# Seven block products in another order on swapping banks, and the sample rows computed apart from the prompt rows

## The chip, the core and the metric

One core of one Trainium2 chip runs the whole kernel. The metric is device time in microseconds (us) of one execution. Matrix work runs on TensorE (PE), whose weight loads are listed apart (PEld); VectorE (DVE) and ScalarE (ACT) read PSUM and do the elementwise work; nearly all DMA is issued from SyncE's queue (SP).

## What is computed

One layer of a hybrid decoder, for a prompt of 2048 tokens and for 8 sample tokens (one new token of each of 8 sequences, with a cache of 2048 positions):

```
h = rms_norm(x)                               # 1024 wide
q, k, v of three dilated attention groups, 8 heads of 64      = h @ w_in[...]
att = softmax over the groups' lse of the groups' outputs, times silu(gate)
HGRN2 branch: f, q, i of 8 heads of 128 = h @ w_in[...]; a chunked scan; RMSNorm; silu gate
merged = sigmoid(ga) * (att @ w_att_proj) + sigmoid(gb) * (ho @ w_hg_proj)
y = rms_norm(x + merged @ w_out)
```

The outputs are y of the prompt and of the samples, the last keys and values, and the scan's states. Everything is float32.

## The kernel before, in words

**Projections.** All columns of w_in are projected with a Strassen form: a block of 1024 tokens (half of the prompt) by 1024 channels, times 1024 channels by two column blocks, is split in quarters and made of seven products in place of eight. The seven sums of token quarters (A11, A12, A22 and S1 to S4) are kept in SBUF for a whole half as `Hh` and `Hl` (make_H, L192); the matching sums of weights are made for each pair of column blocks by w_combos (L216). For accuracy every operand is split in a rounded part and a remainder (split_w, L188: L189 on ACT, L190 on DVE), and each product takes three matmuls per 128 channels. `ORDER` (L46) is the order in which PE takes the products; some are added up in one PSUM bank, so that a partial sum must be copied out (keep_c, ACT, L369) before the next product is added to the same bank.

**Two kinds of block.** V and I columns come out token-major (nat_block, L259: 5 blocks per half, 336 matmuls of 256 columns, L308 to L311). All others come out channel-major in pairs of 128 columns (t_pair, L350: 34 pairs per half, lines L362 to L365). In the first half (p = 0) t_pair runs each product twice, over 256 columns and then over 260, the last four of which are sample tokens: half of the samples are carried as extra columns of each token quarter. In the second half (p = 1) there is one run of 512 columns.

```
45  SETS = (((0, 256), (256, 260)), ((0, 512),))
46  ORDER = ("A11", "A12", "S2", "S3", "S1", "A22", "S4")
```

In t_pair pa takes product 0, is copied, takes 2, is copied, takes 3, is copied, takes 5; pb takes half of product 1 in front of each of the first two copies' successors; pc takes 4 and 6. The sample columns of a result are taken out by L376 or L378. In nat_block the samples are separate float32 matmuls (L267) and stores.

**Order of the work.** In program order, for p = 0: normalise and transpose 8 tiles of 128 prompt tokens and the samples (norm_T, L241; x_tile, L1109), make_H, V block 0, then 8 more tiles which are stored to hscr for the second half, `setup`, then the V blocks 1 and 2 and two I blocks. att_stage (12 pairs of q and k, with the attention of each group beside the next pair), cb_stage (4 pairs; combine; for p = 0 also the samples' attention: samp_qk, samp_score L703, samp_softmax, samp_av L743), hg_stage (8 heads, 2 pairs each). Then merge pairs 4 and 6 of p = 0, make_H for the second half, merge pair 0 of p = 1, and the samples' scan (samp_hg, L1047, and samp_hg_end). The second half repeats from the V blocks: nat_block, att_stage, cb_stage, hg_stage. At the end a flag is reduced (L1184 to L1191), an If block stands for an exact fallback, one last merge pair (6) runs, and two output stages follow (L1266 to L1268, L1300 to L1302).

**What sets the order.** The program's text is the priority. A scheduler lays the instructions of each engine out ahead of time by priority and its own estimate of when inputs are there, and each engine then runs its list strictly in order. The weight sums of t_pair are made with high priority, so they run ahead of the pair that uses them; five raw tiles (`wr`) and 7 (p = 0) or 5 (p = 1) slots of split weights (`wh`, `wl`) hold them. Tiles wait for the earlier owner of their place. PSUM has eight banks: six for products and two for the rest (`ps_side`, px) in the V and I blocks, three and five elsewhere.

## Time and profile before

| | |
|---|---|
| three runs | 3269.86, 3271.39, 3275.21 us (median 3271.39) |
| the profiled execution | 3269.79 us, its span 3268.0 us |
| busy, share of the span | PE 90%, PEld 77%, DVE 58%, ACT 45% |
| instructions | PE 20260, DVE 4622, ACT 3276 |
| mean granted TensorE clock | 0.951 |
| DMA | 347.97 MB, 106 GB/s over the span |

Times are read from the start of the span. PE is the engine with the most work, so the question of each stage is when PE isn't busy, and what it then waits for; an idle DVE or ACT costs nothing by itself.

### The profile page before, as it was taken

What the parts mean: (1) busy time and instruction counts of PE and PEld (TensorE: products, weight loads), DVE (VectorE), ACT (ScalarE), POOL (GpSimd) and SP (SyncE); (2) the same over time, 40 slices, a digit from 0 to 9 for tenths busy, and PEclk for the clock granted to TensorE, in tenths of its full rate; (3) what the DMA queues carried; (4) which work ended last, traced back from release to release, by engine and by line L of the source; (5) the groups of instructions that cost most, each with busy time, mean ns of one, the idle gap of its engine ahead of it and who ended that gap; (6) DMA issues with size and microseconds to landing.
All of it is one profiled execution on the core that took longest, in us unless ns stands there. A gap on an engine that the chain in (4) does not pass through costs nothing. (4 is left out here: it accounts for less than half of the span.)

```text
span 3268.0 us, 54030 instructions
## 1 busy us (share of the span) xinstructions
PE 2930.1 (90%) x20260; PEld 2514.7 (77%) x20260; DVE 1882.2 (58%) x4622; ACT 1474.3 (45%) x3276; POOL 2.5 (0%) x8
## 2 busy tenths in 40 slices
PE   5799999998779898963799999999899996999999
PEld 4698887887758898962798766767677775899987
DVE  7344555456856777762444555557777775544444
ACT  5322445444436666642232455445576765211222
POOL 0000000000000000000000000000000000000000
PEclk7899999998989999985899999999999998999999
DMA  3432132215732121137342232225422222755542
GB/s 127 144 130 88 52 86 72 77 57 175 236 123 69 59 78 59 60 109 155 111 146 89 74 86 81 86 73 163 134 72 73 70 80 65 218 153 145 157 141 84
DMA packets 444798, 347.97 MB, mean 106 GB/s; under 512 B 27945, under 2 KB 403194, under 8 KB 444514
## 3 DMA queue, kind: packets, MB, share of 16 engines
q1 hardware_dynamic: 443922, 342.49, 35.1%
q8 instruction: 161, 2.64, 0.3%
q0 software_dynamic: 320, 1.05, 0.1%
q14 instruction: 107, 0.88, 0.1%
q10 hardware_dynamic: 288, 0.92, 0.1%
HBM read 236.34 MB, written 108.54 MB: 106 GB/s over the span
## 5 line engine op out<-in xcount | busy, mean ns | idle before, releaser
L189 ACT ACTIVATE wh<-wr 128x512 fp32r<-128x512 f32 (+1 forms) x546 | 364.2, 682 | 606.0 <-PE pa L364 275.2
L190 DVE TENSOR_TENSOR wl<-wr,wh 128x512 fp32r<-128x512 f32 (+1 forms) x546 | 405.3, 756 | 311.3 <-ACT wh L189 293.1
L362 PE MATMUL pa<-hhS,wh 128*128 128x256 f32 (+2 forms) x808 | 280.6, 347 | 44.8 <-ACT cc L369 42.6
L362 PE MATMUL pa<-hhA,wh 128*128 128x256 f32 (+2 forms) x808 | 274.7, 340 | 40.1 <-ACT cc L369 19.5
L362 PE MATMUL pc<-hhS,wh 128*128 128x256 f32 (+2 forms) x808 | 262.1, 324 | 15.2 <-DVE cc L409 15.2
L364 PE MATMUL pa<-hlS,wh 128*128 128x256 f32 (+2 forms) x808 | 267.8, 331 | 0.0
L365 PE MATMUL pa<-hhS,wl 128*128 128x256 f32 (+2 forms) x808 | 267.5, 331 | 0.2 <-DVE wl L190 0.2
L364 PE MATMUL pa<-hlA,wh 128*128 128x256 f32 (+2 forms) x808 | 266.3, 330 | 0.0
L365 PE MATMUL pa<-hhA,wl 128*128 128x256 f32 (+2 forms) x808 | 265.6, 329 | 0.0
L365 PE MATMUL pc<-hhS,wl 128*128 128x256 f32 (+2 forms) x808 | 261.3, 323 | 0.0
L364 PE MATMUL pc<-hlS,wh 128*128 128x256 f32 (+2 forms) x808 | 260.5, 322 | 0.0
L543 ACT ACTIVATE sc<-sc,stg 128x256 f32<-128x256 f32 (+2 forms) x384 | 171.6, 447 | 111.2 <-DVE stg L541 110.3
L362 PEld LDWEIGHTS pa<-hhS,wh 128*128 128x128 f32 x808 | 156.6, 194 | 82.0 <-ACT cc L369 63.9
L362 PEld LDWEIGHTS pa<-hhA,wh 128*128 128x128 f32 x808 | 156.9, 194 | 64.6 <-ACT cc L369 30.9
L541 DVE CUSTOM_DVE_ANT_0 sc<-px,bt 128x256 f32<-128x256 f32 (+2 forms) x384 | 122.6, 352 | 128.4 <-PE px L521 43.3
L362 PEld LDWEIGHTS pc<-hhS,wh 128*128 128x128 f32 x808 | 155.8, 193 | 30.4 <-issue 12.6
L369 ACT COPY cc<-pa 128x260 f32<-128x260 f32 (+2 forms) x303 | 130.9, 432 | 85.3 <-PE pa L365 84.9
L365 PEld LDWEIGHTS pa<-hhA,wl 128*128 128x128 f32 x808 | 157.1, 194 | 13.1 <-issue 1.2
L364 PEld LDWEIGHTS pa<-hlA,wh 128*128 128x128 f32 x808 | 157.3, 195 | 10.7 <-issue 1.0
L365 PEld LDWEIGHTS pa<-hhS,wl 128*128 128x128 f32 x808 | 156.5, 194 | 11.5 <-issue 1.4
L364 PEld LDWEIGHTS pa<-hlS,wh 128*128 128x128 f32 x808 | 156.5, 194 | 10.1 <-issue 1.5
L364 PEld LDWEIGHTS pc<-hlS,wh 128*128 128x128 f32 x808 | 155.2, 192 | 11.7
(457 smaller groups left out, 7756.2 us busy)
## 6 DMA issues: line engine op xcount, KB each, us to landing
wr<-in_w_in SPq DMA_DIRECT2D x272, 256.0 KB
wr<-in_w_in SPq DMA_DIRECT2D x40, 512.0 KB
vt<-vscr SPq DMA_DIRECT2D x52, 256.0 KB
na<-natt SPq DMA_DIRECT2D x48, 264.0 KB
vscr<-vst SPq DMA_DIRECT2D x48, 256.0 KB
natt<-stg SPq DMA_DIRECT2D x32, 264.0 KB
xt<-in_x_prompt SPq DMA_DIRECT2D x16, 512.0 KB
iscr<-vst SPq DMA_DIRECT2D x32, 256.0 KB
```

The costliest lines, as they stand in the source:

```text
L189: A.activation(out=hi, in_=raw, func=AF.Copy)
L190: V.tensor_tensor(out=lo, in0=raw, in1=hi.bitcast(F32), op=ALU.subtract)
L362: TE.matmul(o, wh[:, k], hi[:, k, off:off + n], start=(first and k == 0), stop=False, skip_group_check=True)
L364: TE.matmul(o, wh[:, k], lo[:, k, off:off + n], start=False, stop=False, skip_group_check=True)
L365: TE.matmul(o, wl[:, k], hi[:, k, off:off + n], start=False, stop=(k == 3), skip_group_check=True)
L369: A.copy(out=c[:, 0:n], in_=ps[:, 0:n])
L541: V.tensor_tensor_reduce(out=sc[:, hx, 0:W], in0=spss[hx][:, 0:W], in1=bt[:, hx, BW - W:BW], scale=-0.125, scalar=3e38, op0=ALU.add, op1=A ...
L543: A.activation(out=sc[:, hx, 0:W], in_=sc[:, hx, 0:W], func=AF.Exp, scale=-1.0, bias=stg[:, u, 128 + hx:129 + hx], accum_out=stg[:, u, 130 ...
```

## The change

The products are taken in another order and spread over the three banks so that a whole other product stands between a bank's copy and its next use; pa and pb swap from pair to pair. Weight sums and make_H follow that order. The samples are no longer columns of the token sums: t_combos (p = 0) projects them with 16 float32 matmuls per pair, whose four partial sums a second small matmul adds (`sel`), and every pair now runs over 512 columns at once. The first V block (nat_first) is made with eight plain products, each tile of tokens as it arrives; the remaining eight tiles are normalised two at a time beside the other four blocks, and A21 stands in S4's place until that block is done. The samples' attention moves from cb_stage to the V blocks of the second half, their scan to the I blocks there. Merge pair 4 of p = 1 moves from cb_stage to the end, ahead of the If block, and the weights of the last pair are made before it. The diff, cut:

```diff
-ORDER = ("A11", "A12", "S2", "S3", "S1", "A22", "S4")
+ORDER = ("A11", "S1", "S2", "A12", "S3", "S4", "A22")
...
+    def make_H(a11, a12, a21, a22, cs):
+        put_h("A11", a11, cs)
+        V.tensor_tensor(out=a11, in0=a11, in1=a21, op=ALU.subtract)
+        V.tensor_tensor(out=a21, in0=a21, in1=a22, op=ALU.add)
+        put_h("S1", a21, cs)
+        put_h("A22", a22, cs)
+        V.tensor_tensor(out=a22, in0=a22, in1=a11, op=ALU.subtract)
+        put_h("S2", a22, cs)
+        put_h("A12", a12, cs)
+        put_h("S3", a11, cs)
+        V.tensor_tensor(out=a12, in0=a12, in1=a22, op=ALU.subtract)
+        put_h("S4", a12, cs)
 
...
         w0 = slot(b11)
-        w1 = slot(b21)
         t3 = pl.tile([P, 4, width], F32, name="wr", tag="wr", bufs=bufs)
         V.tensor_tensor(out=t3, in0=b22, in1=b12, op=ALU.subtract)
         V.tensor_tensor(out=b12, in0=b12, in1=b11, op=ALU.subtract)
+        w1 = slot(b12)
         w2 = slot(b11)
-        w3 = slot(t3)
-        w4 = slot(b12)
+        w3 = slot(b21)
+        w4 = slot(t3)
         V.tensor_tensor(out=b21, in0=b21, in1=b11, op=ALU.subtract)
-        w5 = slot(b21)
-        w6 = slot(b22)
+        w5 = slot(b22)
+        w6 = slot(b21)
         return [w0, w1, w2, w3, w4, w5, w6]
...
+    def samp_rows(pl, raws, width, tag, bufs):
+        ps = ps_side()
+        w2 = 2 * width
+        for c in range(2):
+            for k in range(KT):
+                q = 32 * (k % 4)
+                TE.matmul(ps[q:q + 32, c * width:(c + 1) * width], hs[:, k], raws[k // 4, c][:, k % 4], start=(k < 4),
+                          stop=(k > 3), skip_group_check=True)
+        sp = pl.tile([P, 2 * width], F32, name="sp", tag=tag, bufs=bufs)
+        A.copy(out=sp, in_=ps[:, 0:w2])
+        return sp
...
+    def nat_samp(wn, raws, g, half):
+        sp = samp_rows(wn, raws, 256, "cc", 4)
+        ps = ps_side()
+        TE.matmul(ps[0:NS, :], sel, sp, start=True, stop=True)
+        vs = wn.tile([P, 512], F32, name="vs", tag="cc", bufs=4)[0:NS]
+        V.tensor_copy(vs, ps[0:NS, :])
...
-        for i, t in ((0, pa), (1, pb), (2, pa), (3, pa), (4, pc), (5, pa), (6, pc)):
+        for i, t in enumerate((pa, pc, pa, pb, pa, pc, pa)):
+                prod(t[b], b, i, i in (0, 1, 3))
+                if i < 3:
                     cc[i, b] = keep_c(t[b])
+                    r, c, add = ((0, 0, 0), (1, 1, 1), (0, 1, 2), (1, 0, None))[i - 3]
+                    nat_fin(wn, p, g, half, r, c, b, t[b], None if add is None else cc[add, b])
...
+    def nat_first(wn, units):
+        raws = w_raw(wn, nat_cols(0, 0), 256, 5)
+        names = (("A11", "A12"), ("S4", "A22"))
+        for n in range(8):
+            r, u = n % 2, n // 2
+            units(n)
+            if u % 2 == 0:
+                ps[r, u // 2] = ps_proj(r)
+            for k in range(2):
+                nat_mm(ps[r, u // 2][:, u % 2 * 256:(u % 2 + 1) * 256], Hh[names[r][k]], Hl[names[r][k]], *ws[k],
+                       slice(u * P, (u + 1) * P), u % 2 == 0 and k == 0, k == 1)
+            if u % 2:
+                nat_fin(wn, 0, 0, 0, r, 0, u // 2, ps[r, u // 2], None)
+        ws = [w_slot(wn, raws[k, 1], 256, 3) for k in range(2)]
+        for k in range(2):
+            for b in range(2):
+                for r in range(2):
+                    for u in range(2):
+                        nat_mm(ps[r, b][:, u * 256:(u + 1) * 256], Hh[names[r][k]], Hl[names[r][k]], *ws[k],
+                               slice((2 * b + u) * P, (2 * b + u + 1) * P), u == 0 and k == 0, k == 1)
+                    if k:
+                        nat_fin(wn, 0, 0, 0, r, 1, b, ps[r, b], None)
...
-            pa, pb = ps_proj(0), ps_proj(1)
-            prod(pa, 0, k4, True)
-            c1 = keep_c(pa)
-            prod(pb, 1, k4[:2], True)
-            prod(pa, 2, k4)
-            c2 = keep_c(pa)
-            prod(pb, 1, k4[2:])
-            fin(0, 0, pb, c1)
-            prod(pa, 3, k4)
-            c3 = keep_c(pa)
-            pc = ps_proj(2)
-            prod(pc, 4, k4, True)
-            fin(1, 1, pc, c3)
-            prod(pa, 5, k4)
-            fin(1, 0, pa, None)
-            prod(pc, 6, k4)
-            fin(0, 1, pc, c2)
+            raws = w_raw(pl, c0s, P, nr)
+            if p == 0:
+                sp = samp_rows(pl, raws, P, "sp", 1)
+                ps = ps_side()
+                o = 0 if idx[0] < idx[1] else 1
+                for c in range(2):
+                    e = 8 * (c ^ o)
+                    TE.matmul(ps[:, e:e + 8], sp[:, c * P:(c + 1) * P], sel, start=True, stop=True)
+                i0, i1 = sorted(idx)
+                V.tensor_copy(sampT[:, i0:i1 + 1:i1 - i0], ps[:, 0:16].rearrange("p (c n) -> p c n", c=2))
+            return w_combos(pl, raws, P, nr, slots)
...
+    def t_pair(p, c0s, idx, evs, W=None):
+        f = tp["flip"]
+        tp["flip"] = 1 - f
+        pa, pb, pc = ps_proj(f), ps_proj(1 - f), ps_proj(2)
...
+        prod(pa, 0, True)
+        c1 = keep_c(pa)
+        prod(pc, 1, True)
+        c5 = keep_c(pc)
+        prod(pa, 2)
+        c2 = keep_c(pa)
+        prod(pb, 3, True)
+        evs[0](0, pb, c1)
+        prod(pa, 4)
+        evs[1](1, pa, c5)
+        prod(pc, 5)
+        evs[1](0, pc, c2)
+        prod(pa, 6)
+        evs[0](1, pa, None)
...
-            if p == 0:
-                samp_qk, samp_score, samp_softmax, samp_av, samp_att_end = samp_att_fns(cb)
-                scores = [(g, n) for g in range(3) for n in range(8)]
-                for g in range(3):
-                    samp_qk(g)
             fill = [lambda j=j: att_gates(cb, p, j) for j in (0, 2)]
-            fill += [lambda d=d: merge_pair(cb, p, d) for d in ((0, 2) if p == 0 else (2, 4))]
+            fill += [lambda d=d: merge_pair(cb, p, d) for d in ((0, 2) if p == 0 else (2,))]
...
+        def units(n):
+            r, u = n % 2, n // 2
+            cs = slice(u * P, (u + 1) * P)
             with tc.high_priority(HP):
...
+                a = x_tile(u + 4 * r)
+                put_h(("A11", "S4")[r], a[:, 0:4], cs)
+                put_h(("A12", "A22")[r], a[:, 4:8], cs)
+                if r == 0:
+                    top[0] = a
+            if r == 1:
...
+                t = top[0]
+                sums_H(t[:, 0:4], t[:, 4:8], a[:, 0:4], a[:, 4:8])
+                put_h("S1", a[:, 0:4], cs)
+                put_h("S2", a[:, 4:8], cs)
+                put_h("S3", t[:, 0:4], cs)
+                sto(s4scr[u], t[:, 4:8])
+            if n == 2:
+                x_tile(16)
+
+        nat_first(wn, units)
+        for u in range(0, 4, 2):
+            st = hst()
+            for v in range(2):
+                dma(st[:, 4 * v:4 * v + 4], s4scr[u + v])
+                put_h("S4", st[:, 4 * v:4 * v + 4], slice((u + v) * P, (u + v + 1) * P))
+        for i, (g, half) in enumerate(((1, 0), (2, 0), (3, 0), (3, 1))):
+            nat_block(wn, 0, g, half)
+            for tt in range(8 + 2 * i, 10 + 2 * i):
...
                 st = x_tile(tt)
                 for k in range(2):
                     sto(hscr[k][:, :, (tt - 8) * P:(tt - 7) * P], st[:, 4 * k:4 * k + 4])
...
-        samp_hg_prep, samp_hg, samp_hg_end = samp_hg_fns(mp)
         merge_pair(mp, 1, 0)
-        samp_hg_prep()
         gsm = mp.tile([P, 16, 8], F32, name="gsm")
...
-        for h in range(8):
-            samp_hg(h)
-        samp_hg_end()
...
-        for g, half in ((0, 0), (1, 0), (2, 0), (3, 0), (3, 1)):
-            nat_block(wn, 1, g, half)
+        with pool("sa") as sa:
+            samp_qk, samp_score, samp_softmax, samp_av, samp_att_end = samp_att_fns(sa)
+            scores = [(g, n) for g in range(3) for n in range(8)]
+            for g in range(3):
+                samp_qk(g)
+            for g in range(2):
+                nat_block(wn, 1, g, 0)
+                for _ in range(12):
+                    samp_score(*scores.pop(0))
+            nat_block(wn, 1, 2, 0)
+            samp_softmax()
+            for a in range(2):
+                samp_av(a)
+            samp_att_end()
+        with pool("sh") as sh:
+            samp_hg_prep, samp_hg, samp_hg_end = samp_hg_fns(sh)
+            samp_hg_prep()
+            for half in range(2):
+                nat_block(wn, 1, 3, half)
+                for h in range(4 * half, 4 * half + 4):
+                    samp_hg(h)
+            samp_hg_end()
...
+    ok = nc.values_load(fi[0:1, 0:1], min_val=0, max_val=1)
+    merge_pair(mp, 1, 4)
+    ready = t_combos(1, (merge_cols(1, 6), merge_cols(1, 7)), None)
...
-    ready = t_combos((merge_cols(1, 6), merge_cols(1, 7)), pl=pw, slots=7, raws=5)
     with tc.If(ok < 1):
...
+    merge_pair(mp, 1, 6, ready, G.dma_start)
```

## Rows read from the trace of the kernel before

**Rows 1.** The page, part 1: busy time and share of the span by engine.
```profile
PE 2930.1 (90%) x20260; PEld 2514.7 (77%) x20260; DVE 1882.2 (58%) x4622; ACT 1474.3 (45%) x3276; POOL 2.5 (0%) x8
```

**Rows 2.** Windows, one per stage: length, busy by engine (instructions), PEclk, DMA share, GB/s.
```profile
0.00:73.00 73.00, 36.24 (x201) 30.62 (x202) 53.02 (x109) 44.98 (x92) 0.20 (x4) 0.76 0.33 115
73.00:115.00 42.00, 40.89 (x325) 40.33 (x326) 16.32 (x22) 13.28 (x21) 0.00 (x0) 0.93 0.46 150
115.00:154.00 39.00, 18.05 (x113) 12.59 (x111) 18.57 (x45) 18.80 (x37) 0.00 (x0) 0.70 0.47 137
154.00:309.00 155.00, 155.00 (x1342) 151.37 (x1342) 67.07 (x78) 42.47 (x60) 0.00 (x0) 0.99 0.33 108
314.00:758.00 444.00, 435.31 (x3699) 366.80 (x3700) 233.17 (x744) 212.47 (x655) 0.00 (x0) 0.99 0.26 74
758.00:967.00 209.00, 157.32 (x954) 129.49 (x953) 145.91 (x370) 76.99 (x144) 0.00 (x0) 0.84 0.63 194
967.00:1384.00 417.00, 384.49 (x3056) 372.35 (x3055) 310.78 (x849) 267.03 (x572) 0.00 (x0) 0.98 0.21 64
1386.00:1481.00 95.00, 68.93 (x449) 62.55 (x448) 51.56 (x73) 41.50 (x76) 0.00 (x0) 0.91 0.34 108
1481.00:1575.00 94.00, 24.67 (x144) 14.86 (x144) 27.62 (x75) 23.09 (x68) 0.00 (x0) 0.52 0.66 144
1575.00:1777.00 202.00, 201.26 (x1680) 200.77 (x1680) 86.28 (x85) 57.52 (x75) 0.00 (x0) 0.99 0.34 115
1782.00:2232.00 450.00, 439.80 (x2796) 312.07 (x2797) 239.95 (x661) 221.28 (x614) 0.00 (x0) 1.00 0.29 83
2232.00:2354.00 122.00, 110.33 (x463) 84.02 (x461) 98.12 (x243) 66.60 (x102) 0.00 (x0) 0.97 0.55 172
2354.00:2742.00 388.00, 367.78 (x1850) 294.77 (x1851) 290.05 (x694) 269.97 (x482) 0.00 (x0) 1.00 0.22 68
2742.00:2786.00 44.00, 22.35 (x90) 17.51 (x89) 20.29 (x48) 10.57 (x16) 1.76 (x3) 0.73 0.42 121
```

**Rows 3.** Waits of PE: who waited for whom, us in total, times, longest.
```profile
PE pa L362 <- ACT cc L369: 62.2, 56, 5.2
PE px L1058 <- DVE sv L1055: 52.5, 8, 8.6
PE pb L362 <- DVE cc L409: 22.2, 6, 14.3
...
PE pp L362 <- ACT wh L189: 19.0, 1, 19.0
PE pc L362 <- DVE cc L409: 15.2, 12, 3.0
```

**Rows 4.** Windows with PE never idle, columns as in rows 2.
```profile
1600.00:1680.00 80.00, 80.00 (x680) 80.00 (x679) 34.72 (x34) 23.36 (x30) 0.00 (x0) 1.00 0.39 131
1400.00:1407.20 7.20, 7.20 (x59) 6.94 (x58) 4.15 (x8) 2.46 (x6) 0.00 (x0) 1.00 0.88 328
1464.00:1480.00 16.00, 16.00 (x70) 12.97 (x70) 4.09 (x8) 6.75 (x19) 0.00 (x0) 1.00 0.34 85
183.90:185.64 1.74, 1.74 (x33) 0.78 (x32) 0.86 (x2) 0.36 (x1) 0.00 (x0) 1.00 0.01 4
```

**Rows 5.** Groups by line, 758:967: busy us, mean ns, idle before.
```profile
L749 PE MATMUL px<-vc,ptS 128*32 128x512 f32 x48 | 20.4, 756 | 5.2 <-DMA vc<-in_cache_kv_w 4.9 <-DVE ptS L731 0.3
...
L707 DVE TENSOR_TENSOR kc<-kc,qb 128x512 f32<-128x512 f32 x24 | 16.4, 685 | 10.0 <-DMA qb<-qs_scr 9.9
```

**Rows 6.** Groups by line, 1481:1575, columns as in rows 5.
```profile
L1058 PE MATMUL px<-sv,qss 128*32 128x128 f32 x128 | 21.0, 421 | 52.5 <-DVE sv L1055 52.5
```

**Rows 7.** The chain that ended last, 2740:2790: start us, us, what.
```profile
2758.41 3.98 DMA wr<-in_w_in
...
2764.44 0.80 PE pp L362
```

**Rows 8.** Waits of PE in 2354:2742, columns as in rows 3.
```profile
PE pa L362 <- ACT cc L369: 11.2, 14, 1.5
```

More of the change, by code (lines that the diff above doesn't have):

```diff
@@ L104, in body @@
     kscr = [[dt_(f"kscr{g}{j}", [P, (128, 512, 1024)[g]]) for j in range(4)] for g in range(3)]
+    s4scr = [dt_(f"s4scr{u}", [P, 4, P]) for u in range(4)]
     hscr = [dt_(f"hscr{k}", [P, 4, HALF]) for k in range(2)]
@@ new lines, in nat_fin, with nat_mm @@
+    def nat_fin(wn, p, g, half, r, c, b, ps, add):
+        v = wn.tile([P, 2, 256], F32, name="vst", tag="vst", bufs=2)
+        vf = v.rearrange("p u c -> p (u c)")
+        if add is None:
+            A.copy(out=vf, in_=ps)
+        else:
+            V.tensor_tensor(out=vf, in0=ps, in1=add, op=ALU.add)
+        nat_store(p, g, half, r, c, b, v)
+    def nat_mm(o, hi, lo, wh, wl, us, first, last):
+        for k in range(4):
+            TE.matmul(o, hi[:, k, us], wh[:, k], start=(first and k == 0), stop=False, skip_group_check=True)
+            TE.matmul(o, hi[:, k, us], wl[:, k], start=False, stop=False, skip_group_check=True)
+            TE.matmul(o, lo[:, k, us], wh[:, k], start=False, stop=(last and k == 3), skip_group_check=True)
@@ L301, in prod, with nat_block @@
+    def nat_block(wn, p, g, half):
+        raws = w_raw(wn, nat_cols(g, half), 256, 5)
+        if p == 0:
+            nat_samp(wn, raws, g, half)
+        W = w_combos(wn, raws, 256, 5, 3)
         def prod(ps, b, i, first):
-            hi, lo = Hh[ORDER[i]], Hl[ORDER[i]]
-            wh, wl = W[i]
             for u in range(2):
-                us = slice((2 * b + u) * P, (2 * b + u + 1) * P)
-                o = ps[:, u * 256:(u + 1) * 256]
-                for k in range(4):
-                    TE.matmul(o, hi[:, k, us], wh[:, k], start=(first and u == 0 and k == 0), stop=False,
-                              skip_group_check=True)
-                    TE.matmul(o, hi[:, k, us], wl[:, k], start=False, stop=False, skip_group_check=True)
-                    TE.matmul(o, lo[:, k, us], wh[:, k], start=False, stop=(k == 3), skip_group_check=True)
+                nat_mm(ps[:, u * 256:(u + 1) * 256], Hh[ORDER[i]], Hl[ORDER[i]], *W[i],
+                       slice((2 * b + u) * P, (2 * b + u + 1) * P), first and u == 0, True)
@@ new lines, in t_combos, with prod, keep_c @@
+            return w_combos(pl, raws, P, nr, slots)
+    def t_pair(p, c0s, idx, evs, W=None):
+        W = W or t_combos(p, c0s, idx)
+        pl = tp["p"]
+        f = tp["flip"]
+        tp["flip"] = 1 - f
+        pa, pb, pc = ps_proj(f), ps_proj(1 - f), ps_proj(2)
+        def prod(ps, i, first=False):
+            hi, lo = Hh[ORDER[i]], Hl[ORDER[i]]
+            wh, wl = W[i]
+            for k in range(4):
+                TE.matmul(ps, wh[:, k], hi[:, k], start=(first and k == 0), stop=False, skip_group_check=True)
+                TE.matmul(ps, wh[:, k], lo[:, k], start=False, stop=False, skip_group_check=True)
+                TE.matmul(ps, wl[:, k], hi[:, k], start=False, stop=(k == 3), skip_group_check=True)
+        def keep_c(ps):
+            c = pl.tile([P, 512], F32, name="cc", tag="cc", bufs=3)
+            A.copy(out=c, in_=ps)
+            return c
+        prod(pa, 0, True)
[12 more added lines that the diff above has]
+        evs[0](1, pa, None)
@@ L781, in cb_stage @@
                 combine(cb, j, (2 * p, 2 * p + 1))
-                if p == 0:
-                    for _ in range(6):
-                        samp_score(*scores.pop(0))
-            if p == 0:
-                samp_softmax()
-                for a in range(2):
-                    samp_av(a)
-                samp_att_end()
     def hg_stage(p):
@@ L1228, in body @@
         act = load_act(srcs, *tchunks[0], split=split_v)
-    with pool("ml") as ml_:
-        merge_pair(ml_, 1, 6, W=ready, pl=pw, sto=G.dma_start, nb=2)
+    merge_pair(mp, 1, 6, ready, G.dma_start)
+    mst.close()
+    close_T()
+    bk.__exit__(None, None, None)
+    bk = banks(4)
+    bk.__enter__()
     ph1.close()
```

287 lines of the change are left out of this document (107 added, 180 removed).

## The prediction, made before the changed kernel ran

> **What bounds the kernel now.** I read the page's first part, then one window per stage, then PE's waits, then short windows in which PE never rests. PE is busy 90% of the span [rows 1], so the kernel is a queue of PE work with holes, and each stage is judged by its holes. [Rows 2] has one line per stage; length less PE's busy time is the hole. The V and I blocks have none once they run (155.0 of 155, 201.3 of 202), the attention stages nearly none (435 of 444, 440 of 450). The holes are: the start (37 of 73 us, then 21 of 39 while the second eight tiles are normalised), the first combine stage (52 of 209; its twin in the second half has 12 of 122), the first scan stage (33 of 417), the merge pairs (26 of 95), the samples' scan (69 of 94, with the clock at 0.52, half speed) and the end (22 of 44). [Rows 3] says on what: 62.2 + 22.2 + 15.2 = 100 us on copies and sums that must leave a bank before the next product enters it, 52.5 us on the samples' scan, 19.0 us on weights at the end.
>
> **The sum** is made against the profiled execution, 3269.8 us, which lies 1.6 us under the median of the three runs, so 1.6 is added at the end.
>
> **A pair of columns, p = 0.** [Rows 4] give the rates at full clock: 680 matmuls of 256 columns in 80 us, 0.118 us each; 59 of 260 columns in 7.2 us, 0.122; 70 of 512 columns in 16.0 us, 0.229, of which the edges count one too many, so 0.231. A pair took 84 x 0.118 + 84 x 0.122 = 20.2 us and will take 84 x 0.231 = 19.4. The gain of halving the weight loads is thus 0.8 us a pair, not a factor, since those loads already run beside the matmuls. The added sample rows are 32 instructions of 128 columns. In the V blocks 32 of 256 columns take 1.74 us [rows 4], so 0.9 us here; the adding matmuls, the copy's hand-over and the two breaks in the stream have no row, and I take 0.6, between nothing and the whole path from a landed weight tile to PE (rival C). Net: 20.9 us against 20.2. The copies to sampT that this removes lie on DVE, which isn't the bound.
>
> [...]
>
> **Start, 0 to 314: -39.** Today block 0 needs all eight tiles and their sums for its first product; its last five products fill 73 to 115, then 39 us pass over eight tiles, then four blocks run without a hole. After: eight tiles still arrive at the pace of DVE and ACT, which were busy 53 and 45 of 73 us [rows 2], and half of the plain products fit in PE's holes there. I put their end at 67 us. The other half is 192 x 0.118 = 23 us, the samples 2.6: 92. Four blocks are 4 x (336 x 0.118 + 2.6) = 169; the transposes of eight tiles beside them at most the 18 us that PE was busy in 115 to 154 at a lower clock, at full clock some 9: 270, and 5 us to the first pair as today (309 to 314): 275. The plain block itself costs 48 matmuls more, 5.7 us, which is in this. Bounds: 260 if the ramp ends at 55; 295 if the new tiles' loads, now on SP's queue between the blocks' weights and stores, hold up PE.
>
> **First attention, 314 to 758: +4.** 12 x 0.7 = 8, less about half of the 9 us of holes. The five px banks get two more users per pair; bounds 0 and +20.
>
> **First combine, 758 to 967: -81.** The twin in the second half does the same four pairs, the combine and the first scan pair in 122 us without the samples' attention [rows 2]. Five pairs' sample rows add 7.5, better copies take 1.5: 128.
>
> **First scan, 967 to 1384: -16.** The twin takes 388, and 377 without the 11.2 us of copy waits that [rows 8] shows in it; 16 pairs' sample rows add 24: 401. There half a product, 6 x 0.231 = 1.4 us, covers a copy, and 14 waits of 0.8 us on average, 1.5 at most, remain; in the new order a whole product, 2.8 us, covers each, and a new pair starts on the bank that was done three products earlier. Next late is the weights' split, which is a pair ahead.
>
> **Merge pairs and samples' scan, 1386 to 1575: -97.** The scan (94 us) leaves. Of the 26 us of holes before it, 14.3 is one wait on a result's sum queued in DVE behind make_H [rows 3]. make_H still has 11 passes over the whole half on DVE and now waits for A22, the last product of the pair before, so I leave 12. Then 83 us, and 9 to load the first V weights as today: 92 for 189.
>
> **V and I blocks of the second half, 1575 to 1782: +60.** They take 207 with PE full and now carry the samples. PE: 48 instructions of 512 columns for the cached values [rows 5]; a 256-column group of four costs 0.215 us in [rows 4], so at full clock 5 us if four go side by side, 20 if each goes as its load lands; I take 20, the loads being paced by DMA. The scan's 128 instructions were busy 21.0 us at half clock [rows 6], 10 to 14 at full. Transposes, softmax and small matmuls: 10. Together 43. DMA: 209 x 0.63 - 122 x 0.55 = 65 us of all engines' time for the attention, 94 x 0.66 = 62 for the scan, 202 x 0.34 = 69 for the blocks [rows 2]: 196 us in some 260, so it fits with little to spare. SP's queue takes 72 loads of the attention and 16 loads and 8 large stores of the scan among the blocks' own; POOL's keeps only the last pair's stores, as today. What is late next is a weight load behind a store that waits on SP, or an in-order matmul behind a sample load. I take 17 for that and for the tail of the last four heads, whose tiles the second attention's need. DVE's 86 busy plus 33 for the scores (two passes of the 16.4 in [rows 5]) and 28 for the scan are covered. Bounds +25 and +115 (rival A).
>
> **Second half.** Attention: 0, its copies never were late. Combine: 122 less a pair of 19.4: -19. Scan: -11 [rows 8]. End, 2742 to 2786: today 22 us of hole and one pair, of which 19.0 us on weights that are loaded only after the If block [rows 3]. After: two pairs, 39, and of the hole I leave 6 for the If block, which still stops every engine: 45, +1. Bounds: -5, or +15 if the weights wait again.
>
> Sum: -39 + 4 - 81 - 16 - 97 + 60 + 0 - 19 - 11 + 1 = -198; 3269.8 - 198 + 1.6 = 3073 us. Own range 3035 to 3110, from the bounds of the start, the sample rows and the moved work.
>
> **Rivals.**
> A, the moved work isn't hidden: PE runs in order and waits for sample loads and DVE steps as it did in their own places. All of it would give back 81 + 94 = 175 in place of 60: 3188; half of the difference 3130. For: the scan's stage used 0.66 of the DMA engines for little data, and PE waited eight times, 6.6 us each. Against: 196 of 260. Chance of half or more: 0.13.
> B, the copies' waits aren't removed but change names (weights, px banks, evacuations on ACT): the change then doesn't do what it says. About 48 us of the sum rest on them (11 in the second scan, 25 in the first, 12 at the merge pairs): 3121. For: DVE and ACT are busy 75% and 70% of the second scan. Against: a whole product now covers each copy. 0.08.
> C, slower: the sample rows read raw weights that may have just landed, in PE's in-order queue. If the scheduler's estimate of a load is too short, every one of the 34 pairs of p = 0 stops for a landing and the way to PE: 2758.41 to 2764.44 is 6.0 us for the last pair today [rows 7]. 34 x 6.0 = 204: 3277. It decides from 5.8 us a pair. For: weight sums in DVE now wait for PE too. Against: the V blocks' sample matmuls read raw weights in the same way today, inside a stretch without a hole [rows 2]. 0.04.
> D, better: cached values in fours (-15), sample rows at 0.9 us (-20), no stalls in the blocks (-14): 3024. 0.12.
> [...]
>
> **How the numbers follow.** The forecast has 0.62, A 0.13, D 0.12, B 0.08, C 0.04, E 0.01. 3010 to 3140 holds the forecast, D, B and half of A. A measurement of this kernel tells 0.2%, 6.5 us, from no change. Only C ends there or above: slower 0.03, same 0.01, faster 0.96.
>
> **What would show it.** Right: no window like 1481 to 1575 and a clock near 1.00 there; the first combine stage at about 128 us; `pa <- ACT cc` under 15 us in PE's waits; 512-column pairs at 0.231; the first pair before 280; V and I blocks at 250 to 270 with PE over 90% busy. Wrong: PE waits on `wr` landings or on `sp`; PE waits on `sv`, `vc` or `wh` in those blocks; DMA share near 1 there.

## The result and the profile after

The changed kernel takes 3174.09 us (median of four runs, 3172.90 to 3182.43) against 3270.62 for the kernel before (four runs): a ratio of 0.971, 95% interval 0.969 to 0.973. The forecast was 3073, its range ended at 3140: 101 us too low. The profiled execution of after is the slowest of the four, 3182.43 us, 8 above the median; its stages are compared with the profiled 3269.8 of before.

Windows of after, one per stage, columns as in [rows 2]. They answer to those rows in the same order, but the start has three lines in place of four, and the samples' scan, which has no stage of its own any more, has none.

```profile
0.00:58.00 58.00, 44.30 (x334) 41.14 (x338) 43.70 (x86) 41.63 (x80) 0.20 (x4) 1.00 0.56 182
58.00:121.00 63.00, 62.22 (x537) 58.27 (x530) 29.33 (x37) 21.47 (x34) 0.00 (x0) 1.00 0.40 130
121.00:265.00 144.00, 139.19 (x1182) 131.30 (x1180) 62.37 (x86) 53.53 (x85) 0.00 (x0) 0.99 0.46 144
265.00:757.00 492.00, 460.45 (x3096) 327.90 (x3088) 220.24 (x663) 207.24 (x612) 0.00 (x0) 0.93 0.22 65
757.00:885.00 128.00, 112.94 (x599) 89.53 (x599) 99.20 (x246) 73.57 (x108) 0.00 (x0) 0.95 0.52 164
885.00:1343.00 458.00, 412.61 (x2429) 342.81 (x2429) 302.00 (x718) 273.48 (x483) 0.00 (x0) 0.92 0.20 60
1343.00:1429.00 86.00, 70.64 (x339) 54.16 (x331) 58.01 (x66) 39.69 (x55) 0.00 (x0) 0.94 0.41 134
1429.00:1711.00 282.00, 253.44 (x1873) 224.59 (x1873) 142.36 (x220) 81.62 (x151) 0.00 (x0) 0.94 0.67 196
...
1738.00:2174.00 436.00, 425.72 (x2729) 301.65 (x2728) 230.98 (x648) 213.70 (x602) 0.00 (x0) 1.00 0.29 82
2174.00:2281.00 107.00, 87.55 (x375) 69.19 (x373) 88.86 (x232) 51.61 (x80) 0.00 (x0) 0.92 0.57 177
2281.00:2651.00 370.00, 355.61 (x1861) 299.40 (x1861) 290.37 (x700) 276.32 (x490) 0.00 (x0) 1.00 0.24 74
2651.00:2699.00 48.00, 40.08 (x162) 31.94 (x161) 23.03 (x54) 15.40 (x25) 1.21 (x2) 0.93 0.35 111
```

Two lines are out of place. The first attention stage (492) and the first scan stage (458) are *longer* than before (444 and 417 in [rows 2]) although the copies' waits shrank. In both PE stands idle more (31.5 and 45.4 us, against 9 and 33) and the granted clock is 0.93 and 0.92, where it was 0.99 and 0.98. The next view says on what PE waits in after, in the whole span, to be laid beside [rows 3]; the line behind it is the kernel before's for the softmax wait, in the same view.

```profile
PE px L891 <- DVE eb L852: 38.5, 7, 5.5
PE px L681 <- issue: 21.6, 8, 5.9
PE px L591 <- ACT sc L581: 20.0, 44, 0.8
PE pb L416 <- ACT cc L422: 13.2, 7, 2.0
PE px L618 <- ACT ot L615: 12.5, 16, 1.1
PE pa L322 <- ACT cc L339: 12.0, 2, 7.2
...
PE pa L416 <- DVE cc L449: 8.3, 2, 7.2
...
PE px L255 <- DMA wr<-in_w_in: 5.6, 4, 4.2
```

```profile
PE px L553 <- ACT sc L543: 11.1, 28, 0.8
```

The 100 us on copies and sums are down to some 34 (the three `cc` lines). In their place stand waits inside the side work (the attention's or the scan's own small steps beside a pair's products), between the steps of a softmax (L591, 0.5 us each on average; L618, 0.8) or on the scan's decay (L891, 5.5). The waits of L618 on `ot` and of L891 on `eb` have no counterpart in the kernel before. Such a wait shows when PE has nothing else to do while another engine does its step. For the wait of L681, in the two combine stages, the profile names no cause; it stands at 21.3 and 17.8 us in the experiments e1 and e12 below too, so it isn't part of what follows.

So the question is what took that other work away. DVE's own waits in 265:757, a view that the prediction had not listed, name it: the in-place weight sums (L238) wait for the sample rows (L255), twelve times for twelve pairs.

```profile
DVE wr L238 <- PE px L255: 47.3, 12, 4.9
```

In the kernel before, in 314:758, the sums never wait for PE but, nearly always, for loads (L227):

```profile
DVE wr L227 <- DMA wr<-in_w_in: 7.4, 8, 1.8
```

In the first scan the same view reads otherwise, in after (885:1343):

```profile
DVE wr L237 <- DMA wr<-in_w_in: 31.5, 14, 5.2
...
DVE wr L238 <- PE px L255: 2.2, 9, 0.2
```

and in the kernel before (967:1384):

```profile
DVE wr L227 <- DMA wr<-in_w_in: 6.0, 12, 0.9
```

There the wait for the rows itself is small, and the sums wait for the next pair's loads instead. Late rows and sums hold the five raw tiles that these loads need. That this is the path in the scan fits the lines, and e9 below, where the rows don't read these tiles, has 5.0 us of this wait there; it was not tried by itself.

The timeline of PE around the end of one pair's side work (start us, us, what, idle before):

```profile
503.36 0.66 PE L618 MATMUL px<-cm,ot 128*128 128x128 f32 x4 [1.06 <-ACT ot L615]
...
505.42 0.42 PE L591 MATMUL px<-cm,sc 128*64 128x128 f32 x1 [0.78 <-ACT sc L581]
...
512.17 0.48 PE L618 MATMUL px<-cm,ot 128*128 128x128 f32 x1 [0.69 <-ACT ot L615]
512.58 1.94 PE L255 MATMUL px<-wr,hs 128*32 128x128 f32 x32
514.44 0.90 PE L618 MATMUL px<-cm,ot 128*128 128x128 f32 x3
515.14 0.89 PE L400 MATMUL px<-cm,sp 128*128 128x8 f32 x4
515.88 0.77 PE L416 MATMUL pc<-hhS,wh 128*128 128x512 f32 x1
...
517.91 0.63 PE L417 MATMUL pc<-hlS,wh 128*128 128x512 f32 x1
518.34 0.63 PE L418 MATMUL pc<-hhS,wl 128*128 128x512 f32 x1
```

The rows of the *next* pair come at the very end of the side work, and its second product (`pc`) only after them. Only the first product, whose weights are the raw ones, ran earlier (up to 499). Windows over the same place show the granted clock:

```profile
494.00:504.00 10.00, 8.79 (x103) 5.87 (x101) 2.61 (x22) 6.34 (x27) 0.00 (x0) 1.00 0.30 74
504.00:514.00 10.00, 8.14 (x94) 5.34 (x97) 2.88 (x17) 3.63 (x15) 0.00 (x0) 0.54 0.37 97
514.00:521.00 7.00, 7.00 (x31) 5.16 (x24) 5.61 (x10) 3.12 (x6) 0.00 (x0) 0.50 0.32 81
521.00:531.00 10.00, 10.00 (x44) 8.19 (x43) 3.60 (x6) 2.22 (x4) 0.00 (x0) 0.96 0.28 80
```

Within the side work, where PE runs small matmuls and stands idle for 12 and 19% of the first two windows, the granted clock falls from 1.00 to 0.54. In the third it is 0.50, and the next product pays: its matmuls start 0.43 us apart (517.91, 518.34 in the timeline), against 0.23 in the last window (44 in 10.0 us, at 0.96).

**Theory T1.** `samp_rows` takes a px bank, and px banks are given out in program order. The next pair's `t_combos` stands *behind* `att_side` (and `hg_side`), so its rows get a bank after all side work. Three of the weight sums overwrite tiles that the rows read, so they wait too, and six of seven products with them, since DVE and PE take theirs in order. Nothing is left to fill the side work's latencies. **R1**: the rows' PE work itself costs it. **R2**: the new order of the products leaves too little to fill with.

### The profile page after: what moved, and what is told of

Read it like the earlier page. It is cut to its first block, busy times and chain, and to the rows that moved or that the text cites. A ratio compares the mean times of both kernels' runs of the same rounds, so it can differ in the third digit from the quotient of the medians.

```text
span 3180.6 us, 49982 instructions
## 1 busy us (share of the span) xinstructions
PE 2957.3 (93%) x18686; PEld 2413.2 (76%) x18686; DVE 1829.4 (58%) x4303; ACT 1466.2 (46%) x3084; POOL 2.5 (0%) x8
## 5 line engine op out<-in xcount | busy, mean ns | idle before, releaser
L416 PE MATMUL pc<-hhS,wh 128*128 128x512 f32 x544 | 225.0, 414 | 8.3 <-ACT wh L191 3.8
L418 PE MATMUL pc<-hhS,wl 128*128 128x512 f32 x544 | 225.2, 414 | 5.2 <-DVE wl L192 5.1
L417 PE MATMUL pc<-hlS,wh 128*128 128x512 f32 x544 | 222.0, 408 | 0.0
L416 PE MATMUL pa<-hhA,wh 128*128 128x512 f32 x408 | 165.2, 405 | 12.9 <-DVE cc L449 8.3
L416 PE MATMUL pb<-hhA,wh 128*128 128x512 f32 x408 | 166.4, 408 | 5.2 <-PEq L1277 3.9
L417 PE MATMUL pb<-hlA,wh 128*128 128x512 f32 x408 | 164.6, 403 | 0.0
L418 PE MATMUL pb<-hhA,wl 128*128 128x512 f32 x408 | 163.3, 400 | 0.0
L417 PE MATMUL pa<-hlA,wh 128*128 128x512 f32 x408 | 163.0, 399 | 0.0
L418 PE MATMUL pa<-hhA,wl 128*128 128x512 f32 x408 | 162.4, 398 | 0.0
L591 PE MATMUL px<-cm,sc 128*128 128x128 f32 (+1 forms) x600 | 132.6, 299 | 21.2 <-ACT sc L581 20.0
L591 PEld LDWEIGHTS px<-cm,sc 128*128 128x128 f32 (+1 forms) x600 | 65.1, 138 | 93.7 <-ACT sc L581 55.7
L416 PE MATMUL pb<-hhS,wh 128*128 128x512 f32 x272 | 110.7, 407 | 13.2 <-ACT cc L422 13.2
```

The source lines that it names most:

```text
L416: TE.matmul(ps, wh[:, k], hi[:, k], start=(first and k == 0), stop=False, skip_group_check=True)
L417: TE.matmul(ps, wh[:, k], lo[:, k], start=False, stop=False, skip_group_check=True)
L418: TE.matmul(ps, wl[:, k], hi[:, k], start=False, stop=(k == 3), skip_group_check=True)
L591: TE.transpose(pt[0:kw, (hx * nw + w) * P:(hx * nw + w + 1) * P], sc[:, hx, w * kw:(w + 1) * kw], ident)
```

## The experiments

This table gives each kernel's stages, cut at the first pair, the first matmul of the scan's side work, the scan's last transpose, the first V-block product, and the same for the second half, in us of each profiled run. "Rest" ends at PE's last matmul, some 7 us before the span's end. From after on it is the same code in every row; it reads 522 to 528, so stage differences under some 5 us say nothing.

```
kernel          start att+comb scan merge blocks att+comb2 scan2 rest  median
before            314    653   417   191   207     573     388   519    3270
forecast          275    576   401    92   267     554     377   520    3073
after             265    620   458    86   282     571     369   522    3174
e1_early          267    582   393    86   284     564     378   527    3089
e2_own_bank       265    597   401    81   284     562     375   527    3106
e3_no_rows        264    544   367    79   281     563     372   522    3006
e4_few_rows       266    629   445    84   281     562     372   527    3176
e5_early_bank     265    598   402    82   288     561     376   526    3108
e6_scan_back      266    586   393   181   247     553     378   528    3142
e7_old_first      289    580   397    86   280     565     368   523    3102
e8_old_order      268    580   401    85   270     583     388   525    3110
e9_untied         266    565   387    83   283     567     373   526    3059
e10_cc5           266    583   393    86   285     566     378   522    3090
e11_old_order     265    582   401    82   266     572     389   526    3097
e12_free_sums     266    563   402    76   281     563     374   525    3061
e13_early_free    265    565   396    86   281     571     374   522    3068
e15_free_nat      267    565   398    84   271     568     371   525    3056
e16_best          266    564   406    77   271     570     374   525    3056
```

### Place, bank or work (e1 to e4, on the changed kernel)

**e1_early**

```diff
...
+                        W = att_combos(p, j, g) if p == 0 else None
                         att_side(at, *pend)
-                        nxt = (p, j, g) + att_proj(at, p, j, g)
+                        nxt = (p, j, g) + att_proj(at, p, j, g, W)
...
+                W = t_combos(p, (merge_cols(0, h), OFF_HG + h * P), (52 + h, 40 + h)) if p == 0 else None
                 hg_decay(h, *t)
                 ss = hg_side(h, *t)
-                hg_gate(h, t[3], ss)
+                hg_gate(h, t[3], ss, W)
```

> The weights, sample rows and weight sums of the next pair are asked for before the side work of the pair before it instead of behind it (p = 0 alone: attention pairs and the gate pairs of the scan). Same instructions, another place in the program's order. T1 (the sample rows take a px bank in program order, so they land behind all side work, the weight sums wait for them, and PE has one product of 12 matmuls to fill with): the first attention falls from 490 to about 445 us and the first scan from 458 to about 405, the time to 3075 to 3090. R1 (the rows' own PE work costs it, wherever it stands): 3174, no change. R2 (the new order of the seven products leaves too little to fill with): 3174, no change.

Measured 3089.06, ratio to before 0.945 (0.943 to 0.947): 85 us below the changed kernel with the same instructions. R1 and R2 fall.

**e2_own_bank**

```diff
-    bk = banks(3, ABC)
+    bk = banks(3, ABC, 1)
...
-        ps = ps_side()
+        ps = ps_samp()
```

> Program order as in the changed kernel, but in the first half the sample rows have a PSUM bank of their own, and the side work four px banks in place of five. T1: the rows no longer queue behind the side work's banks, so the sums of the next pair run early and the time falls as in the run with the early order, to 3075 to 3110, the higher end if four banks pinch the side work. If the place comes from the scheduler's order of the instructions and not from the banks: no gain, 3174 or a little more. R1 and R2: 3174 or more.

Measured 3106.23 (0.951; 0.949 to 0.952): 68 us below, program order untouched. It is the bank that placed the rows. Now they run early, and PE's waits show what that costs in this form (the line that names the rows, L260 here):

```profile
PE py L260 <- DMA wr<-in_w_in: 27.5, 51, 4.3
```

This is rival C's wait for a landed tile: 0.5 us a time and 0.8 us a pair, where rival C had 6.0.

**e3_no_rows**

```diff
-                sp = samp_rows(pl, raws, P, "sp", 1)
...
-                V.tensor_copy(sampT[:, i0:i1 + 1:i1 - i0], ps[:, 0:16].rearrange("p (c n) -> p c n", c=2))
+                V.memset(sampT[:, i0:i1 + 1:i1 - i0], 0.5)
```

> The pairs' sample rows, their adding matmuls and their copies are left out, and a constant stands in sampT, so the samples' outputs that come from the pairs are not computed. This prices all that the rows cost, work and place. T1: about 100 us for the place and 34 x 1.8 = 61 for the work at most, so 3015 to 3060. R1: the same fall, but all of it work, so that the early order above gains nothing. R2: only the work goes, 3115 to 3125.

Measured 3006.09 (0.920; 0.919 to 0.922), below the range that T1 gave. The rows cost 168 us in all in the changed kernel.

**e4_few_rows**

```diff
-            for k in range(KT):
+            for k in range(KT if width > P else 4):
...
```

> The sample rows of a pair shrink from 32 matmuls to 8, which still read all four weight tiles, write the same bank and are followed by the same copy and adding matmuls; the samples' projections are so left out in most parts. The place in the order stays, three quarters of the matmuls go. T1: only work goes, 34 x 24 matmuls x about 0.03 us = 25 us, so 3145 to 3160. R1: about three quarters of what leaving all rows out gains, so 3055 to 3090.

Measured 3175.63 (0.972; 0.970 to 0.973): no change at all. Three quarters of the matmuls are worth nothing as long as the tie stands; even T1 had given them 25 us. They lie in time in which PE would have waited anyway.

### Moves and orders (e5 to e8, on top of the early order)

**e5_early_bank** joins the two edits above.

> The early order and the own bank of the two runs before, together (first half alone). If both mend the same thing, the place of the rows, the second adds nothing: 3080 to 3100, against 3089 with the early order alone. If five px banks for rows and side work were a limit of their own, which the prediction bounded at 0 and +20 in the first attention: 3065 to 3078. If four px banks pinch the side work: over 3100.

Measured 3107.93: 19 us above the early order alone, nearly all in att+comb (598 for 582) and scan (402 for 393). The two mend the same thing. The time came out where the expectation put pinched side work, but PE's waits don't show that: in the first attention and combine its waits between softmax steps fall (0.8 us, 4.4 in e1), while its waits on landed tiles rise to 29.2 us in the whole run, from 5.8 in e1. With a bank of their own the rows run so early that PE waits for their loads.

**e6_scan_back**

```diff
         merge_pair(mp, 1, 0)
+        samp_hg_prep()
...
+        for h in range(8):
+            samp_hg(h)
+        samp_hg_end()
     close_T()
```

> On top of the early order: the samples' scan goes back behind the merge pairs, ahead of the V blocks of the second half, as in the kernel before; the samples' attention stays beside the blocks. Prices that one move. By the prediction's terms the scan alone takes 94 us there, and the blocks get shorter by the scan's 10 to 14 us of matmuls and the 17 us put down to its tail, some 30: 3089 + 64 = 3153. If the blocks lose much more to the scan (28 us of holes and a lower clock stand there): they shorten by 60 to 80 and the time is 3105 to 3125. If the blocks are held by transfers whatever stands beside them: 3175 or more.

Measured 3141.72, 53 above e1. In its own place the scan costs 95 (merge 181 for 86); beside the blocks and the first second-half pairs it costs 48 (284 to 247, 564 to 553). The forecast's 64 was 11 too much. What is left, 247 against 207 of before, is 40 us for the samples' attention together with whatever the new order costs in these blocks (10 to 18 us by e11, e15 and e16, with the scan beside them).

**e7_old_first**

```diff
-        nat_first(wn, units)
...
+            for u in range(4):
+                a, b = x_tile(u), x_tile(u + 4)
+                make_H(a[:, 0:4], a[:, 4:8], b[:, 0:4], b[:, 4:8], slice(u * P, (u + 1) * P))
...
+        nat_block(wn, 0, 0, 0)
```

> On top of the early order: the first V block goes back to seven products behind all eight tiles, as in the kernel before; the second eight tiles stay between the blocks. The start lost 49 us with the change (314 to 265). If the plain first block is what did it: 3089 plus 30 to 50. If the spreading of the second eight tiles over the blocks did it (39 us passed over them in the kernel before): 3089 plus 10 to 20.

Measured 3102.00, 13 above e1. In the profiled run the first pair comes at 289, not 267: of the start's 49 us the plain block gave some 22, the spreading of the second eight tiles the other 27. Of the 22 only 13 reach the whole time; the second scan of this profiled run is 10 shorter (368 for 378), and why was not followed up.

**e8_old_order, e11_old_order**

```diff
-ORDER = ("A11", "S1", "S2", "A12", "S3", "S4", "A22")
+ORDER = ("A11", "A12", "S2", "S3", "S1", "A22", "S4")
```

with the sums, banks and copies to match. In e8 the last two evacuations of a pair stand exchanged, so two quarters of a pair's result are put in each other's place; e11 has them right.

> On top of the early order: the seven products and their banks go back to the kernel before's order (second product split around the third, no swapping of banks), still at 512 columns and with the rows as they are. Prices the order alone, which the prediction put at about 48 us in all (11 in the second scan, 25 in the first, 12 at the merge pairs). If that stands: 3089 + 35 to 50 = 3124 to 3139, the second scan back from 370 to about 385 us. Rival B (the waits only change names): 3089 to 3100.

> The order of the kernel before on top of the early order once more, with the last two evacuations in their right places (in the run before they were exchanged). Expected from that run: 3105 to 3115, so 16 to 26 us for the new order in place of the 48 of the prediction, and V and I blocks of the second half that are some 14 us shorter with the old order, not longer.

Measured 3109.99 and 3096.77, the first between its two ranges, the second below its own; where the 13 us between them lie (att+comb2, 583 and 572) was not followed up. By e11 the new order is worth 8 us in all. By the profiled stages the new order gains 8 in the first scan, 8 in att+comb2 and 11 in the second scan, and loses 18 in the blocks of the second half. PE's waits of e11 in its first scan, 848:1249, show that the *old* order has few waits on copies left there:

```profile
PE pa L414 <- ACT cc L420: 5.2, 7, 0.8
PE pa L414 <- ACT kt L834: 2.3, 7, 0.3
```

and the same view of the kernel before, in 967:1384:

```profile
PE pa L362 <- ACT cc L369: 23.5, 15, 2.7
PE pc L362 <- DVE cc L409: 7.9, 7, 1.1
```

So the old order loses most of them, 5.2 us for 31.4, without the new one. A pair's products run once over 512 columns there in place of twice over 256 and 260, which came from putting the sample rows apart; that the width did it is likely, but it was not tried alone. Over the whole span the copies of the pairs cost no less in the new order (e1):

```profile
PE pb L416 <- ACT cc L422: 25.5, 15, 2.1
```

than in the old (e11):

```profile
PE pa L414 <- ACT cc L420: 24.1, 26, 2.9
```

### The tie (e9, e12, e13) and the blocks (e10, e15, e16)

**e9_untied**, on the changed kernel, program order and banks as there:

```diff
-                TE.matmul(ps[q:q + 32, c * width:(c + 1) * width], hs[:, k], raws[k // 4, c][:, k % 4], start=(k < 4),
+                src = raws[k // 4, c][:, k % 4] if other is None else other[:, k % 4, c * width:(c + 1) * width]
+                TE.matmul(ps[q:q + 32, c * width:(c + 1) * width], hs[:, k], src, start=(k < 4),
...
-                sp = samp_rows(pl, raws, P, "sp", 1)
+                sp = samp_rows(pl, raws, P, "sp", 1, Hh["A11"].bitcast(F32))
```

> The changed kernel in its own program order, with five px banks, but the sample rows of the pairs read a resident tile (A11's high part) in place of the pair's weights, so that nothing that changes the weights in place has to wait for them; the samples' projections are so computed from other data. Same matmuls, same place, same banks; only the tie between rows and weight sums is gone. If the harm is that the sums wait for rows that come late (T1's second link): 3085 to 3110, near the early order. If the rows' late place alone does it: 3160 to 3175.

Measured 3058.82 (0.935; 0.933 to 0.937): 115 below the changed kernel and below both ranges, with the rows as late as ever. It is the tie: what waits for the late rows. The gap to e3 is the rows' bare work: 53 us over 34 pairs, 1.55 us a pair.

**e12_free_sums**, on the changed kernel:

```diff
+        def minus(a, b, old):
+            d = pl.tile([P, 4, width], F32, name="wr", tag="wr", bufs=bufs) if apart else old
+            V.tensor_tensor(out=d, in0=a, in1=b, op=ALU.subtract)
+            return d
...
-        V.tensor_tensor(out=b12, in0=b12, in1=b11, op=ALU.subtract)
+        b12 = minus(b12, b11, b12)
...
-            return w_combos(pl, raws, P, nr, slots)
+            return w_combos(pl, raws, P, nr, slots, p == 0)
...
-    open_T(7, 5)
+    open_T(6, 7)
```

> The changed kernel in its own program order, rows reading the pair's own weights, but the sums of a pair's weights go to buffers of their own instead of over the weights (ring of 7 raw tiles, 6 split slots in place of 5 and 7, the same memory), so six of the seven products' weights no longer wait for the rows. If the tie is what costs, as the untied rows showed with other data: 3055 to 3090, the higher end if late rows hold the raw tiles and with them the next loads. If the reading of just landed weights costs (rival C): 3130 or more. If it is only that the rows come late: 3160 to 3175.

Measured 3061.48 (0.937; 0.935 to 0.938), with the true data and the same memory. Its timeline of PE at the end of a pair's side work, to be laid beside the one of after:

```profile
484.41 0.60 PE L623 MATMUL px<-cm,ot 128*128 128x128 f32 x4
485.38 0.47 PE L421 MATMUL pc<-hhS,wh 128*128 128x512 f32 x1
486.17 0.39 PE L421 MATMUL pa<-hhS,wh 128*128 128x512 f32 x1
...
492.65 1.08 PE L260 MATMUL px<-wr,hs 128*32 128x128 f32 x32
```

The rows still come last, but the next pair's second and third products (`pc`, then `pa`) run before them, among the side work. Windows of its first attention and first scan:

```profile
266.00:735.00 469.00, 466.01 (x3232) 335.09 (x3228) 249.43 (x728) 230.19 (x642) 0.00 (x0) 0.99 0.28 82
735.00:829.00 94.00, 87.29 (x501) 69.70 (x499) 78.18 (x197) 55.98 (x86) 0.00 (x0) 0.98 0.53 164
829.00:1231.00 402.00, 385.97 (x2421) 321.26 (x2422) 294.68 (x710) 288.20 (x499) 0.00 (x0) 0.99 0.22 68
```

Beside after: attention and combine together 563 us with PE busy 553, where it was 620 with 573; the scan 402 with 386, where it was 458 with 413. Of the 113 us, 66 are idle time and 47 a busy time that shrank for the same work, with the clock back at 0.98 to 0.99. An estimate from these windows, busy time times what the clock lacks of 1.00, gives 71 us in after and 10 here, so the clock can account for all of the 47.

**e13_early_free** joins e1 and e12.

> Both mends: the early order and the sums in buffers of their own. The early order alone stands at 3089, the untied rows at 3059, no rows at 3006; 34 pairs x 1.5 us of rows make 51 of the 53 between the last two. If what is left of the tie (30 us) goes: 3055 to 3068. If those 30 us are the rows' wait for a landing, which the untied rows didn't have either: 3080 to 3090.

Measured 3068.30, not better than e12: once the sums are free, the place is of no account. Of the 30 us between e1 and e9, 21 were the rest of the tie. For the other 9 the rows' wait for a landing, which e9 doesn't have, is not ruled out.

**e10_cc5**

```diff
-            c = wn.tile([P, 512], F32, name="cc", tag="cc", bufs=4)
+            c = wn.tile([P, 512], F32, name="cc", tag="cc", bufs=4 + p)
```

> On top of the early order: in the V and I blocks of the second half the kept copies have five buffers in place of four. With the new order six copies of a block are alive at once, so a copy waits for a buffer that DVE's next sum frees, and DVE stands behind score passes that wait for loads (one such wait on PE is 8.7 us, another 4.6). If the buffers are the cause: the blocks shorten by 8 to 15 us, 3074 to 3081. If DVE's queue alone is (the copy would be late by any number of buffers): 3086 to 3090.

Measured 3090.25, blocks 285: nothing in the time. Of e1, PE, ACT and DVE around the wait that the edit aimed at:

```profile
1405.19 0.69 DVE L749 TENSOR_TENSOR kc<-kc,qb 128x512 f32<-128x512 f32 x1
1405.80 0.68 DVE L317 TENSOR_TENSOR vst<-pb,cc 128x512 f32<-128x512 f32 x1
...
1406.57 0.58 ACT L339 COPY cc<-pa 128x512 f32<-128x512 f32 x1 [12.68 <-DVE vst L317]
...
1407.21 0.58 PE L322 MATMUL pa<-wh,hhS 128*128 128x256 f32 x1 [8.65 <-ACT cc L339]
```

PE waits for a copy, the copy for a sum, and the sum stands on DVE behind score passes that wait for their loads. One more buffer does shorten PE's waits on these copies (5.6 us for 13.2), but the wait for the scan's tiles `sv` takes part of it back (13.6 for 9.8), and the blocks don't get shorter. Six copies are alive at once; six buffers were not tried.

**e15_free_nat** (on e13) and **e16_best** (on e12) give the V and I blocks the old order, the pairs keep the new one:

```diff
-        W = w_combos(wn, raws, 256, 5, 3)
+        W = nat_combos(wn, raws, 256, 5, 3)
...
-                nat_mm(ps[:, u * 256:(u + 1) * 256], Hh[ORDER[i]], Hl[ORDER[i]], *W[i],
+                nat_mm(ps[:, u * 256:(u + 1) * 256], Hh[ORDER_N[i]], Hl[ORDER_N[i]], *W[i],
```

> The run before with the V and I blocks' seven products in the kernel before's order, and the pairs in the new order. The run with the old order everywhere had these blocks at 265 us against 284, and everything else some 25 us slower. If the two parts are independent: 12 to 19 us below the run before this one. If the pairs need the blocks' order, or the difference was of that run alone: the same time within 5 us.

> The sums in buffers of their own, program order as in the changed kernel, with the V and I blocks' products in the kernel before's order. Sums alone 3061; the blocks' order gave 12 on top of the early order. If the two are independent: 3045 to 3052. If the blocks' order pays only with the early order: 3058 to 3064.

Measured 3055.83 (0.935; 0.933 to 0.936) and 3056.23 (0.935; 0.933 to 0.937). The blocks fall to 271 in both, and in e15 PE's waits on copies in them to 0.3 us, from 11.1 in e13. On e13 the whole gains 12; on e12 5, between its two ranges, which the intervals do not tell from nothing. Both beat the kernel before by 6.5% and the changed one by 118 us.

## Why the prediction was wrong

**The step that failed** is "First attention: +4" together with the rows' part of "First scan: -16". It came out at +44 for attention and combine over the forecast's 576, all of it in the attention, and +57 over 401: together 101 of the 109 us by which the profiled run missed. The step priced the rows as PE work, "The five px banks get two more users per pair; bounds 0 and +20", and never asked in which order those banks are handed out, nor what the in-place sums behind them hold up. "Next late is the weights' split, which is a pair ahead" no longer held: with the rows behind the side work, the sums of the next pair came late too. The work itself was right: 1.5 us a pair forecast, 1.55 measured. With the tie gone (e12) the two stages read 563 and 402 against 576 and 401, and the whole 3061 against 3073. Most of the signs given for being right came true all the same (128 us, the first pair at 265, `pa <- ACT cc` at 12.0, 512 columns in 0.227 us): none of them looks at what DVE waits for.

**Rival C** had the sentence, "weight sums in DVE now wait for PE too", but hung it on landings at 6.0 us in PE's queue. The landings cost 5.6 us in all in after, and some 0.8 a pair where the rows run early (27.5 us in e2, 29.2 in e5). Its evidence against, that the V blocks' rows do the same inside a stretch without a hole, was a false comfort: in after the sums wait there too, 34.6 us for the rows before 265, but PE has a whole block to run meanwhile (busy 139 of 144 us in 121:265); in the attention it has only side work, whose steps wait on one another.

**Copies.** The forecast gave 48 us to the new order: 11 in the second scan, 25 in the first, 12 at the merge pairs. e1 against e11 gives 11, 8 and none, and 8 us net: rival B in size. The waits of the first half fell without the new order. The 11 of the second scan, whose width did not change, are luck: its waits on copies are fewer, 7 for 14, but sum to 13.2 us where [rows 8] has 11.2. What went there are waits on other names, 9.7 us on `qt`, `wh` and `kn` in the kernel before and 0.4 in after, and 12 us of busy time (355.6 for 367.8), for which no run shows the cause.

**Start: -39** came out at -49, its two causes now split (e7: 22 and 27). Its 9 us for the transposes at full clock take the clock of 115 to 154 as half; [rows 2] has 0.70 there, which makes it some 13. **First combine** came out at its 128 us, and **merge** at 86 for 92. **V and I blocks: +60** came out at +75, and the second attention and combine, which take the scan's tail, at 571 for 554 (without the scan, e6 against e1, they are 11 shorter). In the blocks both parts were short: PE idle 28.6 of 282 us where 5.7 of 207 were, so 23 for the 17 taken, and busy 253.4 where 201.3 were, so 52 for the 43, at a clock of 0.94 where full speed was counted. That is rival A by less than a third of its way. The old order of the products would have saved 10 to 18 here (e11, e15, e16), so with it the moved work costs 59 to 64 against the 60; with it PE's two waits on copies, 11 to 13 us, are gone from the blocks.

**Rival E**, a faster stream of 512 columns (chance 0.01), is shown by no run: in 521:531 of after 44 such matmuls in 10.0 us, at a granted clock of 0.96, are 227 ns each, where the forecast took 231 from [rows 4].

## What to carry to other kernels

A new reader of a buffer that is then overwritten in place ties the overwriting to the reader's turn. Price not only its work but whatever waits for the overwritten data, and look for the reader's place in every ring (a set of buffers given out in turn) that it draws from: here the slots went out in program order (e1, e2). Filler for a stage whose steps wait on one another can be worth more than the stage's holes: here 66 us of holes and 47 us of busy time, with the granted clock at 0.98 to 0.99 for 0.92 to 0.95; and a stage that gets longer with fewer waits on the old names should be read in the waits of the engine that is *not* the bound.

## What the runs showed of the hardware

The clock's share was not expected: 47 of the 113 us that the tie cost in two stages are busy time for the same work, which the lower granted clock can account for (0.92 to 0.95 in after, 0.98 to 0.99 in e12). Within one pair the clock falls from 1.00 (494:504) to 0.54 (504:514) and 0.50 (514:521), though PE was busy for 88% of the window before the fall, with small matmuls; it is back at 0.96 (521:531) behind a window in which PE was never idle. What sets it there was not tried by itself. And 32 small matmuls in place of 8 cost nothing (3174 and 3176 us) while they lay in time that was lost anyway.
